# A seven-product tile's sixth token operand, high part too, moved 128 bytes; the mixer's order set anew

## The chip, the core and the metric

The kernel runs on one core of a Trainium2 chip. The metric is device time of one execution in microseconds; lower is better. Time is given as the median of three runs, and the profile is that of one further execution.

## What is computed

One decoder layer in float32 on 512 tokens of width 1024: a SwiGLU block, three parallel token mixers (sparse attention in three branches, a gated delta rule, cross-attention into a memory of 256 tokens) with sigmoid gates, and a second SwiGLU block. Cut to what matters here:

```python
def reference(x, mem, ...):
    h = swiglu(rms_norm(x, ffn1_pre_norm), ffn1_w_gate, ffn1_w_up, ffn1_w_down)
    x = x + 0.5 * rms_norm(h, ffn1_post_norm)
    u = rms_norm(x, mix_pre_norm)
    o_nsa, o_dn, o_mem = ...            # three mixers on u @ w_in
    gates = sigmoid(u @ w_branch_gate).reshape(b, s, 3, d)
    merged = (gates[:, :, 0] * (o_nsa @ w_branch_nsa)
              + gates[:, :, 1] * (o_dn @ w_branch_dn)
              + gates[:, :, 2] * (o_mem @ w_branch_mem))
    x = x + rms_norm(merged @ w_out, mix_post_norm)
    h = swiglu(rms_norm(x, ffn2_pre_norm), ffn2_w_gate, ffn2_w_up, ffn2_w_down)
    return x + 0.5 * rms_norm(h, ffn2_post_norm)
```

`swiglu` is `(silu(h @ w_gate) * (h @ w_up)) @ w_down` with a hidden width of 2816, that is 22 tiles of 128.

## The kernel before

Every float32 product is made of three products of rounded halves (`fp32r`): high by high, low by high, high by low (`mm3`, L117 to L119). ScalarE rounds a weight to its high part (L106), VectorE or GpSimd subtracts to get the low part (L109).

The gate and up products of a SwiGLU tile, and most of the branch gates, are done in another way: two blocks of weights against four blocks of tokens by seven products where eight would be plain (`fast_prods`, L424). Such a seven-product tile issues 7 x 12 matmuls of 128 x 128 weights with 256 token columns, all on L436. For each product and each of four slices `k`, three matmuls follow each other: `wh` by `th`, `wl` by `th`, `wh` by `tl`. The order of the products by token operand is 0, 5, 4, 1, 3, 6, 2; operand 6 (`T_T4`) goes with the weight block `S_A22` into the up half.

The weights of a tile (`fset`, `mset`, or the tiles `xth` and `xtl` used again as `fxth`, `fxtl`) begin 16 elements, 64 bytes, into their tile (`OFFW`, L317). The token operands are: the high parts in one tile `thi` of seven blocks of 4096 bytes (L376), the low parts in `txa`, `txb`, `tmth`, two blocks each, and the last one alone in `tmtl`, which begins 32 elements, 128 bytes, into its tile. So operand 6 has its high part at a multiple of 4096 bytes from the start of `thi`, and its low part 128 bytes off. The matmuls of the first SwiGLU block (`fast_phase`, L461, tiles 6 to 21) lie between 71 and 242 us, those of the second one between 1051 and 1210 us.

In the mixer, seven pairs of gate tiles (`pair`, L1421) use the same seven products: three token operands are cut from `uh`, `ul` (`xth`, `xtl`), four are sums made by `token_sums`, in `uhi` (which takes the place of the tile `KA`) with the low parts in `uxa`, `uxb` and `ulo`; `ulo` begins 128 bytes into its tile. In the middle of each pair two branch products of 512 columns are issued (`mid`). Those tiles lie between 792 and 923 us.

What runs between is a list of tasks, issued in the order of a list (`order`, `order2` and so on, read by `tasks`, L1163). `off` gives a task a head start in the scheduler's priorities; `pool` says how many of its loads leave the low part to GpSimd (2 is every second one, 0 none). The ones touched: `i` (projection `in_vs`), `C3` (`cmp_probs`), `M..` (`merge`, a gate, a branch product and their product added into `mg`), `G.` (`mem_q`), `W3`, `S...`, `P...` (pieces of the attention branches), `k0`, `p2` (memory keys, post-norm). Engines work their own queue in order; the scheduler lays the queues out beforehand.

Of the kernel before, what the change touches and what calls it, by code (L numbers as in the profile page):

```python
# [36 lines left out]
PRM = {'order': ['i', 'a', 'w', 'c01', 'h01', 'r0', 'c00', 'c10', 'c02', 'l0', 'h00', 'h02', 'c11', 'c12', 'k0', 'h10', 'c22', 'h12', 'h11', 'c21', 'r1', 'k1', 'l1', 'h21', 'h22', 'b0', 'e0', 'z', 'c20', 'r2', 'h20', 'c32', 'l2', 'c31', 'd00', 'k2', 'h31', 'r3', 'd01', 'l3', 'b1', 'd02', 'x0', 's00', 'e1', 'd10', 'c30', 'h32', 'x1', 'h30', 'd11', 's01', 's02', 's03', 'q3', 'p0', 'd12', 'o0', 'p1', 'k3', 'q0', 'p2', 'p3', 's10', 'p4', 'q1', 'p5', 's11', 'p6', 'p7', 's12', 's13', 'o1', 'q2', 'f'], 'dma': {'l': 'sync', 'b': 'sync', 'd': 'scalar', 'c': 'sync', 'r': 'sync'}, 'off': {'b0': 300, 'h31': 400, 'r1': 50, 'h32': 50, 'h11': 100, 'h12': 200, 'd10': 100, 'A01': 100, 'A10': 100, 'A11': 50, 'A20': 400, 'A31': 100, 'A21': 20, 'x0': 20, 'x1': 20, 'L': 200, 'S310': 400, 'S001': 400, 'S311': 400, 'A30': 100, 'r0': 400, 'd02': 20, 's11': 100, 'V20': 400, 'l3': 100, 'q1': 20, 'f': 100, 'l1': 50, 'h20': 100, 'h22': 100, 'r3': 50, 'P010': 50, 'y': 100, 'h02': 50, 'S101': 20, 'A00': 100, 'Q0': 50, 'Q1': 200, 'Q2': 50, 'Q3': 50, 'P110': 400, 'V31': 400, 'd01': 200, 'o0': 400, 'p0': 50, 'p2': 400, 'p4': 400, 'p5': 400, 'p6': 400, 'p7': 20, 'b1': 200, 'h01': 100, 'P201': 400, 'e0': 100, 'e1': 100, 'o1': 20, 'q0': 50, 'q2': 20, 'h21': 20, 'd11': 200, 'p3': 400, 'U0': 100, 'c11': 20, 's00': 200, 'P011': 400, 'M14': 200, 'c20': 50, 'k2': 20, 'M03': 20, 'V00': 400, 'V01': 400, 'V10': 400, 'V11': 400, 'V21': 400, 'V30': 400, 'l2': 200, 'h00': 400, 'G0': 20, 'S210': 20, 'P101': 200, 'i': 100, 'G2': 100, 'M11': 20, 'F2324': 200, 'S201': 100}, 'ph': 'e', 'po': 'ss', 'xpd': (0, 1, 2), 'order2': ['K1', 'K0', 'B', 'M10', 'Q0', 'C0', 'Q1', 'S000', 'S001', 'P000', 'C3', 'P001', 'C1', 'S010', 'P010', 'C2', 'S011', 'V00', 'Q2', 'S101', 'S100', 'P011', 'S110', 'V01', 'M12', 'P100', 'W0', 'P101', 'S111', 'Q3', 'P110', 'S200', 'V10', 'P111', 'S210', 'V11', 'P200', 'M14', 'M15', 'S201', 'P201', 'S211', 'W1', 'V20', 'P211', 'P210', 'V21', 'S301', 'W2', 'S300', 'S311', 'P301', 'M11', 'P300', 'L', 'M13', 'S310', 'V30', 'M16', 'G2', 'M17', 'G0', 'P311', 'P310', 'V31', 'W3'], 'order0': ['d0', 'p0', 'n0', 't0', 'd1', 'k2', 'p2', 'k0', 'p3', 'n1', 'v', 'k3', 'k1', 't1'], 'order3': ['s2', 's3', 's7', 's6', 's5', 's1', 's0', 's4', 'd00', 'd01', 'd11', 'g', 'p0', 'd10', 'n0', 'p1', 't0', 'n1'], 't3': (('mm', 'r'), ('e', 's')), 'pool': {'W2': 2, 's13': 3, 'k0': 0, 'k1': 0, 'k2': 0, 'k3': 2, 'p3': 1, 'C0': 1, 'C1': 0, 'C2': 0, 'C3': 2, 'S310': 0, 'L': 3, 'd11': 3, 'p0': 1, 'p1': 1, 'p2': 1, 'p4': 2, 'p5': 1, 'p6': 1, 'p7': 1, 'S311': 0, 'h01': 1, 'h00': 2, 'h02': 0, 'h10': 0, 'h11': 0, 'h12': 0, 'h22': 0, 'h21': 2, 'h20': 0, 'h31': 0, 'h30': 3, 'h32': 0, 'i': 2, 'P011': 2, 'c21': 0, 'd01': 2, 'S000': 0, 'S001': 0, 'S010': 0, 'S011': 0, 'S100': 0, 'S101': 0, 'S110': 0, 'S111': 0, 'S200': 0, 'S201': 0, 'S210': 0, 'S211': 0, 'S300': 0, 'S301': 0, 'M24': 2, 'G2': 2, 'A01': 0, 'M10': 0, 'M15': 2, 'M12': 2, 'M14': 2, 'M13': 2, 'M17': 2, 'M11': 2, 'M16': 2, 'M23': 0, 'M27': 3, 'M01': 2, 'M00': 2, 'M03': 0, 'M07': 2, 'M06': 1, 'M22': 2, 'M04': 2, 'M20': 2, 'M26': 2, 'M02': 0, 'M21': 2, 'M25': 2, 'M05': 2, 'c11': 1, 'o1': 3, 'P000': 2, 'P001': 1, 'P010': 2, 'P100': 2, 'P101': 2, 'P110': 2, 'P111': 2, 'P200': 2, 'P201': 2, 'P210': 2, 'P211': 2, 'P301': 0, 'P300': 3, 'P310': 1, 'P311': 2, 'c12': 0, 'b1': 1, 'x0': 0, 'x1': 0, 'V21': 0, 'c30': 0, 'c01': 0, 'c02': 0, 'c00': 0, 'c10': 0, 'c22': 0, 'c20': 0, 'c31': 3, 'c32': 0, 's01': 3, 'A31': 0, 'd12': 0, 'y': 2, 'G0': 2, 'G1': 2, 'G3': 0, 'U3': 0, 'W3': 2, 'r1': 2, 's12': 3, 'U2': 0, 'Q0': 2, 'Q1': 2, 'Q2': 2, 'Q3': 1, 's00': 3, 's02': 2, 's03': 3, 's10': 2, 's11': 3, 'e1': 2, 'd00': 1, 'U0': 0, 'U1': 0, 'l2': 0, 'd02': 2, 'K1': 3, 'V11': 0, 'V00': 2, 'r2': 0, 'l3': 3, 'T3': 0, 'F0001': 0, 'A21': 3}, 'pool3': {'d00': 3, 'd01': 3, 'd10': 0, 'd11': 0, 'p1': 2, 't1': 3, 't0': 3, 's5': 2, 's7': 2, 's1': 2, 's0': 2, 's3': 2, 's6': 2, 's2': 2, 's4': 2, 'q0': 1}, 'pool0': {'t0': 2}, 'off0': {'p3': 20, 'n1': 50, 'k2': 200, 'k1': 20, 'p2': 100, 'p0': 400}, 'off3': {'s1': 20, 's5': 200, 'g': 50, 't0': 200, 'd10': 200, 'p0': 200, 'n0': 200}, 'tt': ('e', 's'), 'order_s': ['w000', 't00', 'w010', 't01', 'P00', 'w110', 'y', 'w100', 't03', 't02', 'P10', 'w011', 'w001', 'P01', 'w111', 'R0', 'w101', 'F000', 'P11', 'x', 'n', 't10', 't12', 'F200', 't11', 'F101', 't13', 'F110', 'B', 'F211', 'F011', 'c'], 't0': ('e', 's'), 'rs': ((0, 0), (0, 0)), 'ra': (1, 1), 'warm': 8, 'pools': {'F000': 0, 'F101': 0, 'F200': 0, 'F011': 0, 'F110': 0, 'F211': 0, 'w10': 0, 'w11': 1, 't00': 0, 't01': 0, 't02': 0, 't03': 0, 't13': 0, 't10': 0, 't11': 0, 't12': 0, 'w00': 0, 'w01': 0, 'w000': 0, 'P01': 0}, 'ptc': 'vvs', 'cva': 'v', 'offs': {'t13': 100, 'R1': 400, 't03': 20, 't02': 20, 'w001': 100, 'w110': 20, 'R0': 200}, 'vnc': 's', 'sp3': 0, 'hsc': 'vv', 'sf2': 2, 'psc': 'vvvv', 'sp1': 0, 'vbs': 'v', 't1c': 'vs', 'sgv': 256, 'nset': 1, 'order4': ['T0', 'A00', 'A01', 'T1', 'G1', 'T2', 'T3', 'F0001', 'G3', 'M07', 'D0001', 'A10', 'A11', 'F0203', 'A30', 'A31', 'U1', 'D0203', 'U0', 'A20', 'U3', 'A21', 'F0405', 'U2', 'D0405', 'F0620', 'D0620', 'F2122', 'D2122', 'F2324', 'D2324', 'F2526', 'D2526', 'M27'], 'gon2': 0}  # L37


class Body:  # L40
# [1583 lines left out]
```

## Time and profile before

| | us |
|---|---|
| median of three runs | 1339.57 (1331.78, 1339.57, 1341.33) |
| the profiled execution | 1339.93 |
| its span, first to last instruction | 1338.1 |
| TensorE (PE) busy | 1304.5, 97% of the span |
| VectorE (DVE) busy | 960.9, 72% |
| ScalarE (ACT) busy | 739.6, 55% |

PE is TensorE's matmuls, PEld its weight loads. Busy time of PE counts the modelled length of each matmul; matmuls overlap, so the distance from one start to the next tells more than the length. PEclk is the clock that the chip granted, as a share of full speed.

### The profile page before, as it was taken

What the parts mean: (1) busy time and instruction counts of PE and PEld (TensorE: products, weight loads), DVE (VectorE), ACT (ScalarE), POOL (GpSimd) and SP (SyncE); (2) the same over time, 40 slices, a digit from 0 to 9 for tenths busy, and PEclk for the clock granted to TensorE, in tenths of its full rate; (3) what the DMA queues carried; (4) which work ended last, traced back from release to release, by engine and by line L of the source; (5) the groups of instructions that cost most, each with busy time, mean ns of one, the idle gap of its engine ahead of it and who ended that gap; (6) DMA issues with size and microseconds to landing.
All of it is one profiled execution on the core that took longest, in us unless ns stands there. A gap on an engine that the chain in (4) does not pass through costs nothing. (4 is left out here: it accounts for less than half of the span.)

```text
span 1338.1 us, 22370 instructions
## 1 busy us (share of the span) xinstructions
PE 1304.5 (97%) x8091; PEld 1133.7 (85%) x8091; DVE 960.9 (72%) x1857; ACT 739.6 (55%) x1591; POOL 132.0 (10%) x116
## 2 busy tenths in 40 slices
PE   8999999999999999999999999999999999999997
PEld 7889999887887778788777778888888999998886
DVE  6898876768567866846898466566687787766775
ACT  6566665767455644416555345444685556546652
POOL 0020000000012222003120211223100000000000
PEclk9999999999999999999999999999999999999999
DMA  7553331587654341334121331323745433317673
GB/s 239 190 162 117 105 118 42 177 261 240 193 178 131 102 119 45 84 109 130 45 63 40 94 118 57 95 95 114 271 151 161 139 95 112 110 32 268 195 224 108
DMA packets 106302, 178.35 MB, mean 133 GB/s; under 512 B 18780, under 2 KB 28368, under 8 KB 106192
## 3 DMA queue, kind: packets, MB, share of 16 engines
q1 hardware_dynamic: 105904, 176.67, 42.0%
q8 instruction: 63, 1.03, 0.3%
q14 instruction: 47, 0.39, 0.1%
q10 hardware_dynamic: 288, 0.26, 0.1%
HBM read 166.84 MB, written 10.01 MB: 132 GB/s over the span
## 5 line engine op out<-in xcount | busy, mean ns | idle before, releaser
L106 ACT CAST whi<-wraw 128x512 fp32r<-128x512 f32 (+1 forms) x286 | 173.4, 617 | 163.5 <-PE pfm L119 56.5
L109 DVE TENSOR_TENSOR wlo<-wraw,whi 128x512 fp32r<-128x512 f32 (+1 forms) x252 | 172.8, 693 | 77.1 <-ACT whi L106 71.9
L117 PE MATMUL pfm<-xth,whi 128*128 128x512 f32 x272 | 109.3, 404 | 2.5 <-ACT tg L1132 1.4
L118 PE MATMUL pfm<-xth,wlo 128*128 128x512 f32 x272 | 109.3, 404 | 0.5 <-DVE wlo L109 0.5
L119 PE MATMUL pfm<-xtl,whi 128*128 128x512 f32 x272 | 108.1, 400 | 0.0
L106 ACT CAST ringh<-ringr 128x512 fp32r<-128x512 f32 x82 | 49.9, 622 | 41.8 <-DMA ringr<-in_ffn_d_dram 8.9
L436 PE MATMUL smm<-thi,fset 128*128 128x256 f32 x384 | 69.1, 279 | 0.0
L109 DVE TENSOR_TENSOR wlo<-ringr,ringh 128x512 fp32r<-128x512 f32 x75 | 51.4, 690 | 20.8 <-PE acc_e L119 8.0
L109 POOL TENSOR_TENSOR wlo<-wraw,whi 128x512 fp32r<-128x512 f32 (+1 forms) x31 | 42.6, 1375 | 237.3 <-ACT whi L106 138.7
L117 PEld LDWEIGHTS pfm<-xth,whi 128*128 128x128 f32 x272 | 51.1, 188 | 13.7 <-ACT tg L1132 2.2
L456 DVE TENSOR_TENSOR up<-s,smm 128x256 f32<-128x256 f32 x32 | 13.5, 421 | 66.2 <-ACT se L451 66.2
L118 PEld LDWEIGHTS pfm<-xth,wlo 128*128 128x128 f32 x272 | 51.2, 189 | 10.2 <-issue 0.9
L119 PEld LDWEIGHTS pfm<-xtl,whi 128*128 128x128 f32 x272 | 51.1, 188 | 9.2 <-issue 0.4
L436 PEld LDWEIGHTS smm<-thi,fset 128*128 128x128 f32 x384 | 58.4, 188 | 0.2
L436 PE MATMUL smm<-thi,fxtl 128*128 128x256 f32 x192 | 53.7, 280 | 0.6 <-DVE fxtl L411 0.6
L436 PE MATMUL smm<-thi,fxth 128*128 128x256 f32 x192 | 53.5, 279 | 0.0
L436 PE MATMUL se<-thi,fset 128*128 128x256 f32 x256 | 46.0, 279 | 0.0
L1057 ACT ACTIVATE Pm<-Pm,nm 128x128 f32<-128x128 f32 (+1 forms) x64 | 35.7, 560 | 12.8 <-DVE nm L1056 12.5
L123 DVE TENSOR_TENSOR Hl<-H,Hh 128x256 fp32r<-128x256 f32 x88 | 35.0, 421 | 7.0 <-ACT Hh L122 5.4
L402 DVE TENSOR_TENSOR fs<-fq 128x1024 f32<-128x1024 f32 x32 | 39.0, 1220 | 0.1
L436 PEld LDWEIGHTS se<-thi,fset 128*128 128x128 f32 x256 | 38.9, 188 | 0.0
L436 PEld LDWEIGHTS smm<-thi,fxtl 128*128 128x128 f32 x192 | 36.0, 188 | 1.0 <-DVE fxtl L411 1.0
(611 smaller groups left out, 4255.8 us busy)
## 6 DMA issues: line engine op xcount, KB each, us to landing
wraw<-in_ffn_d_dram SPq DMA_DIRECT2D x94, 256.0 KB, 2.8
ringr<-in_ffn_d_dram SPq DMA_DIRECT2D x82, 256.0 KB, 3.0
fq<-in_ffn_g_dram SPq DMA_DIRECT2D x64, 256.0 KB, 2.8
fq<-in_ffn_u_dram SPq DMA_DIRECT2D x64, 256.0 KB, 3.1
wraw<-in_ffn_g_dram SPq DMA_DIRECT2D x34, 256.0 KB, 3.3
wraw<-in_ffn_u_dram SPq DMA_DIRECT2D x34, 256.0 KB, 3.4
woraw<-in_w_out_dram SPq DMA_DIRECT2D x32, 256.0 KB, 3.7
mfq<-in_w_gate_dram SPq DMA_DIRECT2D x28, 256.0 KB, 2.9
```

The source lines that it names most:

```text
L106: nc.scalar.copy(hi, raw)
L109: eng.tensor_tensor(lo, raw, hi.bitcast(F32), op=OP.subtract)
L117: t.matmul(out, lh, rh, start=first, stop=False)
L118: t.matmul(out, ll, rh, start=False, stop=False)
L119: t.matmul(out, lh, rl, start=False, stop=last)
L123: return self.nc.vector.tensor_tensor(lo, src, hi.bitcast(F32), op=OP.subtract)
L402: add = lambda *x: v.tensor_tensor(*x, op=OP.add)
L436: m = lambda x, y, **kw: te.matmul(out, x, y, skip_group_check=True, **kw)
L456: v.tensor_tensor(up[:, 256:], s7, a, op=OP.subtract)
L1057: nc.scalar.activation(pm, pm, AF.Exp, bias=nm[:, qb : qb + 1], scale=-1.0, accum_out=sm[:, qb : qb + 1])
```

## The change

The high part of operand 6 is shifted by 32 elements (128 bytes) as well. `thi` becomes one flat tile with 64 more elements, and its blocks a list. In the mixer the high part of the operand whose low part is `ulo` (number 1 of the four) goes to the end of `uhi`, also 128 bytes off a multiple of 1024; `KA`, whose place it takes, grows by 64 elements, 256 bytes. All that lies behind these tiles in their pools moves by 256 bytes.

```diff
-                nc.scalar.copy(self.thi[:, i], f[i])
-                q = v.tensor_tensor(self.tlo[i], f[i], self.thi[:, i].bitcast(F32), op=OP.subtract)
+                nc.scalar.copy(self.thi[i], f[i])
+                q = v.tensor_tensor(self.tlo[i], f[i], self.thi[i].bitcast(F32), op=OP.subtract)
...
-        self.thi = st.tile([P, 7, 4, 256], F32R, name="thi")
+        thi = st.tile([P, 7 * 1024 + 64], F32R, name="thi")
+
+        self.thi = [thi[:, 1024 * i + i // 6 * 32 :][:, :1024].rearrange("p (k t) -> p k t", k=4) for i in range(7)]
...
-                KA = ap_.tile([P, 8, SEQ], F32R, tag="KA", name="KA")
+                KA = ap_.tile([P, 8 * SEQ + 64], F32R, tag="KA", name="KA")[:, : 8 * SEQ].rearrange("p (k t) -> p k t", k=8)
...
-                        E["hi"] = ap_.tile([P, 4, 4, 256], F32R, tag="KA", name="uhi")
+                        hi = ap_.tile([P, 4 * 1024 + 64], F32R, tag="KA", name="uhi")
+                        E["hi"] = [hi[:, o : o + 1024].rearrange("p (k t) -> p k t", k=4) for o in (0, 3104, 1024, 2048)]
```

The other lines only change `thi[:, i]` to `thi[i]` and `E["hi"][:, k]` to `E["hi"][k]`. The lists of tasks change like this (one dictionary on one line, L37; old above, new below, cut to the neighbours):

```diff
 order2
-'S000', 'S001', 'P000', 'C3', 'P001'
+'S000', 'C3', 'S001', 'P000', 'P001'
-'P110', 'S200', 'V10', 'P111', 'S210', 'V11', 'P200', 'M14', 'M15'
+'P110', 'M14', 'S200', 'V10', 'P111', 'S210', 'V11', 'P200', 'M15'
-'S310', 'V30', 'M16', 'G2', 'M17', 'G0', 'P311', 'P310', 'V31', 'W3'
+'S310', 'G2', 'V30', 'M16', 'G0', 'P311', 'P310', 'V31', 'W3', 'M17'
 order4
-'F0001', 'G3', 'M07', 'D0001'
+'F0001', 'M07', 'G3', 'D0001'
 order0
-'k2', 'p2', 'k0', 'p3'
+'k2', 'k0', 'p2', 'p3'
 pool
-'i': 2
+'i': 0, 'q1': 3, 'o0': 0
 off
-'S310': 400
+'s12': 200, 'P301': 50, 'P311': 200, 'W3': 100
 offs
+'P11': 20
```

No task, matmul, copy or transfer is added or taken away.

## Rows read from the trace of the kernel before

**Rows 1.** The page: busy time, and the granted clock in forty slices.
```profile
PE 1304.5 (97%) x8091; PEld 1133.7 (85%) x8091; DVE 960.9 (72%) x1857; ACT 739.6 (55%) x1591; POOL 132.0 (10%) x116
...
PEclk9999999999999999999999999999999999999999
```

**Rows 2.** L436 by windows: us, PE busy (matmuls), PEld, PEclk, DMA share, GB/s.
```profile
110.00:160.00 50.00, 50.00 (x442) 50.00 (x441) 1.00 0.36 114
1100.00:1150.00 50.00, 50.00 (x427) 50.00 (x427) 1.00 0.33 106
```

**Rows 3.** Timeline, first block: start us, length us, engine, line, out<-in, tile, count.
```profile
151.43 0.39 PE L436 MATMUL smm<-thi,fset 128*128 128x256 f32 x2
151.66 0.28 PE L436 MATMUL smm<-txb,fset 128*128 128x256 f32 x1
151.77 0.39 PE L436 MATMUL smm<-thi,fset 128*128 128x256 f32 x2
...
152.79 0.39 PE L436 MATMUL ss<-thi,fset 128*128 128x256 f32 x2
...
154.19 0.40 PE L436 MATMUL se<-thi,fset 128*128 128x256 f32 x2
...
155.56 0.28 PE L436 MATMUL smm<-thi,fxth 128*128 128x256 f32 x1
...
171.94 0.39 PE L436 MATMUL ss<-thi,fset 128*128 128x256 f32 x2
```

**Rows 4.** Timeline, second block, the same products.
```profile
1136.67 0.40 PE L436 MATMUL smm<-thi,fset 128*128 128x256 f32 x2
...
1138.09 0.40 PE L436 MATMUL ss<-thi,fset 128*128 128x256 f32 x2
...
1139.50 0.40 PE L436 MATMUL se<-thi,fset 128*128 128x256 f32 x2
...
1157.88 0.40 PE L436 MATMUL ss<-thi,fset 128*128 128x256 f32 x2
```

**Rows 5.** Timeline, gate pairs of the mixer, around a break at 890.41.
```profile
890.05 0.40 PE L436 MATMUL dmm<-xth,mset 128*128 128x256 f32 x2
890.29 0.28 PE L436 MATMUL dmm<-xtl,mset 128*128 128x256 f32 x1
890.41 0.68 PE L436 MATMUL de<-xth,mset 128*128 128x256 f32 x2
...
891.73 0.39 PE L436 MATMUL de<-xth,mset 128*128 128x256 f32 x2
...
892.07 0.39 PE L436 MATMUL ds<-uhi,mset 128*128 128x256 f32 x2
...
906.27 0.40 PE L436 MATMUL dmm<-xth,mset 128*128 128x256 f32 x2
...
907.69 0.40 PE L436 MATMUL de<-xth,mset 128*128 128x256 f32 x2
```

**Rows 6.** Timeline, plain products with 256 columns ahead of the second block.
```profile
1002.05 0.28 PE L117 MATMUL pg<-xth,whi 128*128 128x256 f32 x1
1002.17 0.28 PE L118 MATMUL pg<-xth,wlo 128*128 128x256 f32 x1
1002.29 0.28 PE L119 MATMUL pg<-xtl,whi 128*128 128x256 f32 x1
```

**Rows 7.** Waits of PE between 700 and 812 us: us in total, times, longest.
```profile
PE de L436 <- DVE mset L416: 2.1, 1, 2.1
PE pfm L117 <- ACT mq L1294: 1.9, 1, 1.9
PE pfm L117 <- ACT tg L1132: 1.4, 1, 1.4
PE de L436 <- DVE mset L411: 1.2, 1, 1.2
```

**Rows 8.** Timeline around 805 us, ACT and DVE; idle before and its releaser in brackets.
```profile
804.51 1.22 DVE L402 TENSOR_TENSOR msum<-mfq 128x1024 f32<-128x1024 f32 x1 [1.93 <-DMA mfq<-in_w_gate_dram]
805.82 0.62 ACT L415 CAST mset<-msum 128x512 fp32r<-128x512 f32 x1 [2.30 <-DVE msum L402]
807.07 0.59 ACT L1294 ACTIVATE mq<-pfm 128x512 f32<-128x512 f32 x1
807.71 0.50 PE L117 MATMUL pfm<-onh,whi 128*128 128x512 f32 x1 [1.90 <-ACT mq L1294]
```

**Rows 9.** Windows, all engines: us, PE, PEld, DVE, ACT, POOL busy (count), PEclk, DMA.
```profile
385.00:410.00 25.00, 24.96 (x177) 23.29 (x176) 12.18 (x33) 13.86 (x37) 3.76 (x6) 1.00 0.49 145
600.00:700.00 100.00, 99.39 (x556) 77.72 (x555) 80.88 (x248) 62.02 (x170) 23.61 (x19) 1.00 0.28 80
```

**Rows 10.** All matmuls into `smm` and the pairs' `ds`, by tile: duration ns min/median/max, first and last start.
```profile
L436 PE MATMUL smm<-thi,fset x384: 276/281/281, 71.6 to 1197.2; 128*128 128x256 f32 x192
L436 PE MATMUL smm<-thi,fxth x192: 276/281/281, 90.6 to 1207.0; 128*128 128x256 f32 x192
L436 PE MATMUL ds<-uhi,mset x56: 276/281/682, 795.0 to 910.3; 128*128 128x256 f32 x56
```

More of the change, by code (lines that the diff above doesn't have):

```diff
@@ new lines @@
+PRM = {'order': ['i', 'a', 'w', 'c01', 'h01', 'r0', 'c00', 'c10', 'c02', 'l0', 'h00', 'h02', 'c11', 'c12', 'k0', 'h10', 'c22', 'h12', 'h11', 'c21', 'r1', 'k1', 'l1', 'h21', 'h22', 'b0', 'e0', 'z', 'c20', 'r2', 'h20', 'c32', 'l2', 'c31', 'd00', 'k2', 'h31', 'r3', 'd01', 'l3', 'b1', 'd02', 'x0', 's00', 'e1', 'd10', 'c30', 'h32', 'x1', 'h30', 'd11', 's01', 's02', 's03', 'q3', 'p0', 'd12', 'o0', 'p1', 'k3', 'q0', 'p2', 'p3', 's10', 'p4', 'q1', 'p5', 's11', 'p6', 'p7', 's12', 's13', 'o1', 'q2', 'f'], 'dma': {'l': 'sync', 'b': 'sync', 'd': 'scalar', 'c': 'sync', 'r': 'sync'}, 'off': {'b0': 300, 'h31': 400, 'r1': 50, 'h32': 50, 'h11': 100, 'h12': 200, 'd10': 100, 'A01': 100, 'A10': 100, 'A11': 50, 'A20': 400, 'A31': 100, 'A21': 20, 'x0': 20, 'x1': 20, 'L': 200, 'S001': 400, 'S311': 400, 'A30': 100, 'r0': 400, 'd02': 20, 's11': 100, 'V20': 400, 'l3': 100, 'q1': 20, 'f': 100, 'l1': 50, 'h20': 100, 'h22': 100, 'r3': 50, 'P010': 50, 'y': 100, 'h02': 50, 'S101': 20, 'A00': 100, 'Q0': 50, 'Q1': 200, 'Q2': 50, 'Q3': 50, 'P110': 400, 'V31': 400, 'd01': 200, 'o0': 400, 'p0': 50, 'p2': 400, 'p4': 400, 'p5': 400, 'p6': 400, 'p7': 20, 'b1': 200, 'h01': 100, 'P201': 400, 'e0': 100, 'e1': 100, 'o1': 20, 'q0': 50, 'q2': 20, 'h21': 20, 'd11': 200, 'p3': 400, 'U0': 100, 'c11': 20, 's00': 200, 'P011': 400, 'M14': 200, 'c20': 50, 'k2': 20, 'M03': 20, 'V00': 400, 'V01': 400, 'V10': 400, 'V11': 400, 'V21': 400, 'V30': 400, 'l2': 200, 'h00': 400, 'G0': 20, 'S210': 20, 'P101': 200, 'i': 100, 'G2': 100, 'M11': 20, 'F2324': 200, 'S201': 100, 's12': 200, 'P301': 50, 'P311': 200, 'W3': 100}, 'ph': 'e', 'po': 'ss', 'xpd': (0, 1, 2), 'order2': ['K1', 'K0', 'B', 'M10', 'Q0', 'C0', 'Q1', 'S000', 'C3', 'S001', 'P000', 'P001', 'C1', 'S010', 'P010', 'C2', 'S011', 'V00', 'Q2', 'S101', 'S100', 'P011', 'S110', 'V01', 'M12', 'P100', 'W0', 'P101', 'S111', 'Q3', 'P110', 'M14', 'S200', 'V10', 'P111', 'S210', 'V11', 'P200', 'M15', 'S201', 'P201', 'S211', 'W1', 'V20', 'P211', 'P210', 'V21', 'S301', 'W2', 'S300', 'S311', 'P301', 'M11', 'P300', 'L', 'M13', 'S310', 'G2', 'V30', 'M16', 'G0', 'P311', 'P310', 'V31', 'W3', 'M17'], 'order0': ['d0', 'p0', 'n0', 't0', 'd1', 'k2', 'k0', 'p2', 'p3', 'n1', 'v', 'k3', 'k1', 't1'], 'order3': ['s2', 's3', 's7', 's6', 's5', 's1', 's0', 's4', 'd00', 'd01', 'd11', 'g', 'p0', 'd10', 'n0', 'p1', 't0', 'n1'], 't3': (('mm', 'r'), ('e', 's')), 'pool': {'W2': 2, 's13': 3, 'k0': 0, 'k1': 0, 'k2': 0, 'k3': 2, 'p3': 1, 'C0': 1, 'C1': 0, 'C2': 0, 'C3': 2, 'S310': 0, 'L': 3, 'd11': 3, 'p0': 1, 'p1': 1, 'p2': 1, 'p4': 2, 'p5': 1, 'p6': 1, 'p7': 1, 'S311': 0, 'h01': 1, 'h00': 2, 'h02': 0, 'h10': 0, 'h11': 0, 'h12': 0, 'h22': 0, 'h21': 2, 'h20': 0, 'h31': 0, 'h30': 3, 'h32': 0, 'i': 0, 'P011': 2, 'c21': 0, 'd01': 2, 'S000': 0, 'S001': 0, 'S010': 0, 'S011': 0, 'S100': 0, 'S101': 0, 'S110': 0, 'S111': 0, 'S200': 0, 'S201': 0, 'S210': 0, 'S211': 0, 'S300': 0, 'S301': 0, 'M24': 2, 'G2': 2, 'A01': 0, 'M10': 0, 'M15': 2, 'M12': 2, 'M14': 2, 'M13': 2, 'M17': 2, 'M11': 2, 'M16': 2, 'M23': 0, 'M27': 3, 'M01': 2, 'M00': 2, 'M03': 0, 'M07': 2, 'M06': 1, 'M22': 2, 'M04': 2, 'M20': 2, 'M26': 2, 'M02': 0, 'M21': 2, 'M25': 2, 'M05': 2, 'c11': 1, 'o1': 3, 'P000': 2, 'P001': 1, 'P010': 2, 'P100': 2, 'P101': 2, 'P110': 2, 'P111': 2, 'P200': 2, 'P201': 2, 'P210': 2, 'P211': 2, 'P301': 0, 'P300': 3, 'P310': 1, 'P311': 2, 'c12': 0, 'b1': 1, 'x0': 0, 'x1': 0, 'V21': 0, 'c30': 0, 'c01': 0, 'c02': 0, 'c00': 0, 'c10': 0, 'c22': 0, 'c20': 0, 'c31': 3, 'c32': 0, 's01': 3, 'A31': 0, 'd12': 0, 'y': 2, 'G0': 2, 'G1': 2, 'G3': 0, 'U3': 0, 'W3': 2, 'r1': 2, 's12': 3, 'U2': 0, 'Q0': 2, 'Q1': 2, 'Q2': 2, 'Q3': 1, 's00': 3, 's02': 2, 's03': 3, 's10': 2, 's11': 3, 'e1': 2, 'd00': 1, 'U0': 0, 'U1': 0, 'l2': 0, 'd02': 2, 'K1': 3, 'V11': 0, 'V00': 2, 'r2': 0, 'l3': 3, 'T3': 0, 'F0001': 0, 'A21': 3, 'q1': 3, 'o0': 0}, 'pool3': {'d00': 3, 'd01': 3, 'd10': 0, 'd11': 0, 'p1': 2, 't1': 3, 't0': 3, 's5': 2, 's7': 2, 's1': 2, 's0': 2, 's3': 2, 's6': 2, 's2': 2, 's4': 2, 'q0': 1}, 'pool0': {'t0': 2}, 'off0': {'p3': 20, 'n1': 50, 'k2': 200, 'k1': 20, 'p2': 100, 'p0': 400}, 'off3': {'s1': 20, 's5': 200, 'g': 50, 't0': 200, 'd10': 200, 'p0': 200, 'n0': 200}, 'tt': ('e', 's'), 'order_s': ['w000', 't00', 'w010', 't01', 'P00', 'w110', 'y', 'w100', 't03', 't02', 'P10', 'w011', 'w001', 'P01', 'w111', 'R0', 'w101', 'F000', 'P11', 'x', 'n', 't10', 't12', 'F200', 't11', 'F101', 't13', 'F110', 'B', 'F211', 'F011', 'c'], 't0': ('e', 's'), 'rs': ((0, 0), (0, 0)), 'ra': (1, 1), 'warm': 8, 'pools': {'F000': 0, 'F101': 0, 'F200': 0, 'F011': 0, 'F110': 0, 'F211': 0, 'w10': 0, 'w11': 1, 't00': 0, 't01': 0, 't02': 0, 't03': 0, 't13': 0, 't10': 0, 't11': 0, 't12': 0, 'w00': 0, 'w01': 0, 'w000': 0, 'P01': 0}, 'ptc': 'vvs', 'cva': 'v', 'offs': {'t13': 100, 'R1': 400, 't03': 20, 't02': 20, 'w001': 100, 'w110': 20, 'R0': 200, 'P11': 20}, 'vnc': 's', 'sp3': 0, 'hsc': 'vv', 'sf2': 2, 'psc': 'vvvv', 'sp1': 0, 'vbs': 'v', 't1c': 'vs', 'sgv': 256, 'nset': 1, 'order4': ['T0', 'A00', 'A01', 'T1', 'G1', 'T2', 'T3', 'F0001', 'M07', 'G3', 'D0001', 'A10', 'A11', 'F0203', 'A30', 'A31', 'U1', 'D0203', 'U0', 'A20', 'U3', 'A21', 'F0405', 'U2', 'D0405', 'F0620', 'D0620', 'F2122', 'D2122', 'F2324', 'D2324', 'F2526', 'D2526', 'M27'], 'gon2': 0}
@@ L472, in fast_phase @@
         self.fast_load(*gu(f0 + 3), self.sets[1], (quads[1], sums))
-        T = [(self.thi[:, i], self.tlo[i]) for i in range(7)]
+        T = [(self.thi[i], self.tlo[i]) for i in range(7)]
         for f in range(f0 + 2, FT):
@@ L1412, in sum4 @@
                             homes()
-                        self.token_sums(k, uh, ul, E["tt"], E["hi"][:, k], E["lo"][k])
+                        self.token_sums(k, uh, ul, E["tt"], E["hi"][k], E["lo"][k])
                     def gates(br, j, br2, j2):
@@ L1423, in pair @@
                         T = [(q(uh, i, k), q(ul, i, k)) for i, k in ((0, 0), (1, 0), (1, 1))]
-                        T += [(E["hi"][:, k], E["lo"][k]) for k in (0, 1, 3, 2)]
+                        T += [(E["hi"][k], E["lo"][k]) for k in (0, 1, 3, 2)]
                         b = [self.bank(t, "d" + t) for t in ("e", "s", "mm", "o")]
```

1 line of the change is left out of this document (removed).

## The prediction

> **What bounds the kernel now.** I read the page first. PE is busy 97% of the span, and the clock row shows nines in all forty slices [rows 1]; so the kernel ends when TensorE has worked off its list, and a gain must come from faster matmuls or from fewer holes between them. Busy time can't tell the first: I next took the matmuls of L436 by windows. The windows of both SwiGLU blocks are busy for 50.00 of 50.00 us at a granted clock of 1.00 (2.4 GHz), yet the first block gets 442 matmuls into its window and the second one 427 [rows 2]. The same program, the same shapes, 3.5% more time in the second.
>
> The timeline shows where. In the first block three matmuls take 151.77 - 151.43 = 0.34 us, twelve (one product) 152.79 - 151.43 = 1.36 us, that is 113 ns from start to start [rows 3]. In the second block the same product takes 1138.09 - 1136.67 = 1.42 us, 118 ns a matmul [rows 4]. Two speeds, and in neither block is the engine waiting for anything that the profile shows. Nor is it the place of one operand alone: in the gate pairs, the three matmuls up to 890.41 take 0.36 us, then something disturbs the stream (0.68), and from 891.73 to 892.07 three take 0.34; at 906.27 the same product takes 907.69 - 906.27 = 1.42 us again [rows 5]. The stream keeps the step it has fallen into until something jolts it. There is a third step: the plain products of 256 columns, whose weights have no 64-byte offset, go at 1002.17 - 1002.05 = 0.12 us [rows 6]. So where operands lie in bytes seems to matter, and the stream also remembers.
>
> Operand 6, whose low part lies 128 bytes off, is where the two blocks differ least. In the first block its product takes 154.19 - 152.79 = 1.40 us and the next one 155.56 - 154.19 = 1.37, and then the stream is back at 1.36 [rows 3]: some 0.05 us lost per tile. In the second block it takes 1139.50 - 1138.09 = 1.41 us [rows 4], and nothing changes after it. So the half-shifted operand disturbs a quick stream a little, and doesn't free a slow one.
>
> **The change, part by part.** *The shift of operand 6 in the second block.* No instruction is added. With both parts off, all twelve matmuls of that product meet their weights at one new distance in bytes, where before eight did so at the old and four at the new one. Either this knocks the stream out of the 118 ns step at every tile, or not. If it does, a tile costs what it costs in the first block. Two tiles there take 171.94 - 152.79 = 19.15 us, 9.575 each [rows 3]; in the second block 1157.88 - 1138.09 = 19.79, 9.895 each [rows 4]. The difference is 0.32 us. The high weights of `fset` meet `smm` in 384 matmuls, of `fxth` in 192 with one of the two weight parts [rows 10]; with three products of eight such matmuls per tile that is 384 / 24 = 16 tiles of `fset` in both blocks, and as many of the other weight set (whose two parts are counted apart): 16 tiles per block. Gain: 16 x 0.32 = 5.1 us. Bounds: 0 if the stream stays slow.
>
> *The same in the gate pairs.* `ds` takes eight high-part matmuls per pair, 56 in all [rows 10], so seven pairs; a slow one loses the same 0.32. About one of seven goes quick by itself, as after 890.41 [rows 5]. Gain 6 x 0.32 = 1.9 us, bounds 0 and 2.2.
>
> *The shift in the first block.* The stream is quick there already. Operand 6's own product may go to 1.36 (gain 16 x 0.05 = 0.8) or to twelve matmuls at 0.12, 1.44 us (loss 16 x 0.04 = 0.6, by [rows 6]). I take 0, since two thirds of it already run mixed, near the middle. The rival below is that it drops the stream into the slow step.
>
> *The 256 bytes that other tiles move by* (the pairs' weights, the loads ahead of the second block): 64 and 256 bytes are the steps in which the code lays things out, and no row shows what 256 does. If it mattered, every third load ahead of the second block would be the most: of the two tiles in two halves, 2 x 2 x 2 x 24 = 192 matmuls at 0.120 [rows 6], a third gain 0.007, 0.4 us. I take 0 and keep 0.4 both ways.
>
> *The order of the mixer.* PE's work stays; only holes can close or open. Those next to the moved tasks are the four waits between 700 and 812 us, 2.1 + 1.9 + 1.4 + 1.2 = 6.6 us [rows 7]. M17 goes behind W3 and M07 ahead of G3: both put ready matmuls close to the first pair, whose weights come late from VectorE (the waits on `mset`, 3.3 us). But the work they bring there is taken from somewhere else, and their own evictions queue on ScalarE and VectorE ahead of the pair's. The 1.9 us wait shows what can go wrong: the copy of `mq` (G3, 0.59 us) stood on ScalarE behind a cast that waited 2.30 us for `msum`, which had waited 1.93 us for its DMA, and the branch product behind it needed the bank that the copy frees [rows 8]. With G3 later, that copy is no earlier. Bounds: a gain of 6.6 if all four close, a loss of two more waits of the largest size, 4.2. I take a gain of 0.5, near nothing, since most of each wait is one engine's queue that is as long as before.
>
> *The rest.* `i` gives its four GpSimd subtractions to VectorE: in its stretch PE is busy 24.96 of 25 us and VectorE only 12.18 [rows 9], so PE's matmuls hide it; uncovered it would be four of GpSimd's instructions there at 3.76 / 6 = 0.63 us, 2.5 us. C3, M14 and the new head starts lie where PE is 99.39 of 100 us busy [rows 9]: nothing to close, and up to 0.6 to lose or gain. k0 ahead of p2 and P11's head start the same way. Together 0.
>
> **The sum.** 1339.9 (the profiled execution, 1338.1 of it span, 0.4 above the median) - 5.1 - 1.9 - 0.5 = 1332.4 us.
>
> The three runs before lie at 1331.78, 1339.57 and 1341.33. A kernel that can run at two speeds would show such a spread: the lowest is 8.1 us below the mean of the others (1340.45), and 5.1 + 1.9 is 7.0. That is a hint that whole executions go either way already, no proof.
>
> **The rivals.**
>
> *B. The place in bytes decides nothing; the slow step stays.* For it: the half shift leaves the second block slow for all sixteen tiles [rows 4], and a stall, not an operand, freed the pair at 890.41 [rows 5]. Against it: 0.120 against 0.113 between weights at two offsets [rows 3, 6]. Time: 1339.9 - 0.5 = 1339.4. The Trainium skill, "SBUF — State Buffer", section "Who interferes with whom", speaks for this rival: it gives TensorE two independent read ports, one for the moving operand and one for weight loads, and says it waits on no one; by that an address couldn't change the step. The trace agrees only in part, as two steps at one granted clock [rows 2] are more than that page has.
>
> *C. The jolt works in one of the two places.* In the second block only: 1339.9 - 5.1 - 0.5 = 1334.3; in the pairs only, 1337.5. For it: pairs and blocks have their weights at other places, and branch products break the pairs up.
>
> *D. Slower: the first block falls into the slow step.* Its place is operand 6 there. Today the stream leaves that product and is back at 1.36 after one product [rows 3]; if the wholly shifted product hands it on at 118 ns, and nothing frees it, as in the second block [rows 4], sixteen tiles lose 0.32. It decides if the product that follows operand 6 takes 1.41 and not 1.37. With the second block still slow: 1339.9 + 5.1 = 1345.0. For it: both steps sustain themselves. Against it: an operand that lies elsewhere has so far been left behind within one product.
>
> *E. The mixer's order opens waits.* G3's late copy twice holds up a branch product: two more waits of 2.1 us [rows 7], 1339.9 + 4.2 = 1344.1.
>
> **How the numbers follow.** The forecast (both streams freed) 0.45; B 0.29; C 0.12; D 0.08; E 0.06. The forecast's own range is 1326 (all four waits closed) to 1336 (operand 6 at 0.12 in all tiles, some loss in the mixer). The range for 8 in 10 reaches from 1327.5 to 1341.5: it takes in most of the forecast, B and C, and leaves out D, E and the lowest end. About 1% is what a measurement of this kernel can tell from no change: 1326.2 and 1353.0. Below the first lies only the forecast with nearly all of the mixer's 6.6 us: 0.06. Above the second only D and E together with more: 0.02. Within: 0.92.
>
> **What would show it.** Right: 442 matmuls in a 50 us window of the second block as in the first, and a tile of 9.6 us; pairs with three matmuls in 0.34; the first block unchanged. The order's part is seen in the waits of PE around 800 us, in sum between 0 and 11 us against 6.6. Wrong: 427 in the second block (B), 427 in the first (D), or the span moving by more than 3 us between 340 and 790 us, where I count nothing.

## Result, and the profile after

The changed kernel takes 1329.76 us (median of 18 runs, 1324.47 to 1337.19) against 1337.91 us before (18 runs, 1331.78 to 1345.76): a ratio of 0.994, 95% interval 0.9923 to 0.9958, so 8 us less. The forecast was 1332.4 us, 7.5 us below the profiled execution, in a range of 1327.5 to 1341.5. The sum came out close, but not its terms, and the experiments below are about which of them did it. The profiled execution of after took 1327.85 us; its page:

```profile
PE 1299.2 (98%) x8091; PEld 1129.2 (85%) x8091; DVE 959.7 (72%) x1860; ACT 738.6 (56%) x1591; POOL 126.6 (10%) x113
...
PEclk8999999999999999999999999999999999999999
```

The same 8091 matmuls [rows 1]; TensorE is busy 5.3 us less. The lines of `fast_prods` and all below it have moved down by one, so L436 is L437 here. Its matmuls by windows (us, PE busy, PEld, PEclk, DMA share, GB/s):

```profile
110.00:160.00 50.00, 50.00 (x441) 50.00 (x440) 1.00 0.37 116
1100.00:1150.00 50.00, 50.00 (x441) 50.00 (x440) 1.00 0.34 107
```

Against 442 and 427 [rows 2], both blocks now go at the quick step. In the timeline of the second block, one product start each (start us, length us, engine, line, out<-in, tile, count):

```profile
1145.38 0.39 PE L437 MATMUL smm<-thi,fset 128*128 128x256 f32 x2
...
1146.74 0.40 PE L437 MATMUL ss<-thi,fset 128*128 128x256 f32 x2
...
1148.15 0.40 PE L437 MATMUL se<-thi,fset 128*128 128x256 f32 x2
...
1149.52 0.28 PE L437 MATMUL smm<-thi,fxth 128*128 128x256 f32 x1
...
1150.88 0.28 PE L437 MATMUL sr<-thi,fxth 128*128 128x256 f32 x1
```

A product takes 1146.74 - 1145.38 = 1.36 us where it took 1.42 [rows 4]; the shifted one takes 1.41, the next 1.37, and then 1.36 again. That is the picture of the quick stream in the first block before [rows 3], so the whole shift disturbs a quick stream about as the half one did.

The pairs, in the timeline of one of them:

```profile
867.16 0.40 PE L437 MATMUL de<-xth,mset 128*128 128x256 f32 x2
...
868.58 0.40 PE L437 MATMUL ds<-uhi,mset 128*128 128x256 f32 x2
...
872.74 0.40 PE L437 MATMUL de<-uhi,mset 128*128 128x256 f32 x2
872.97 0.28 PE L437 MATMUL de<-ulo,mset 128*128 128x256 f32 x1
...
874.15 0.40 PE L437 MATMUL dmm<-xth,mset 128*128 128x256 f32 x2
...
875.52 0.39 PE L437 MATMUL de<-uhi,mset 128*128 128x256 f32 x2
...
876.88 0.39 PE L437 MATMUL do<-uhi,mset 128*128 128x256 f32 x2
...
878.24 0.40 PE L117 MATMUL pfm<-omth,whi 128*128 128x512 f32 x1
```

In a pair the shifted operand is not number 6 but number 4, the third product, straight behind the first branch product. Ahead of it a product takes 1.42 us, the shifted one (`ulo`) 1.41, and the three behind it 1.37, 1.36, 1.36. Then the second branch product follows, of 512 columns, and behind it the stream is slow again. So three of seven products are quick in each of the six later pairs; in the first one other matmuls stand between the products, and one is quick.

Of the waits of PE between 700 and 812 us [rows 7] none is left. In the stretch of the pairs, 785 to 925 us, one is (us in total, times, longest); it stood there before too, as L1137:

```profile
PE pfm L117 <- DVE tg L1138: 1.4, 1, 1.4
```

Where the time went between the two profiled executions, by the starts of the same matmuls: at the last matmul of the first block after is 0.3 us ahead, at the first matmul of the pairs 1.3, at the last one 8.3, at the first seven-product matmul of the second block 7.9, at its last one 12.7, at the end 12.0. So the pairs gave 7.0 us, 5.2 of it the three waits of [rows 7] that lay in them, and the second block 4.9. The first block gave nothing. The wait for `tg` of 1.4 us, which lay at 744, is gone too, but the stretch from the first block to the pairs got only 1.1 us shorter (550.6 to 549.5).

### The profile page after: what moved, and what is told of

Read it like the earlier page. It is cut to its first block, busy times and chain, and to the rows that moved or that the text cites. A ratio compares the mean times of both kernels' runs of the same rounds, so it can differ in the third digit from the quotient of the medians.

```text
span 1326.1 us, 22368 instructions
## 1 busy us (share of the span) xinstructions
PE 1299.2 (98%) x8091; PEld 1129.2 (85%) x8091; DVE 959.7 (72%) x1860; ACT 738.6 (56%) x1591; POOL 126.6 (10%) x113
## 5 line engine op out<-in xcount | busy, mean ns | idle before, releaser
L437 PE MATMUL smm<-thi,fset 128*128 128x256 f32 x384 | 67.9, 276 | 0.0
L109 POOL TENSOR_TENSOR wlo<-wraw,whi 128x512 fp32r<-128x512 f32 x28 | 38.1, 1360 | 229.2 <-ACT whi L106 165.1
L437 PEld LDWEIGHTS smm<-thi,fset 128*128 128x128 f32 x384 | 57.9, 188 | 0.2
L437 PE MATMUL smm<-thi,fxtl 128*128 128x256 f32 x192 | 53.2, 277 | 0.6 <-DVE fxtl L412 0.6
L437 PE MATMUL smm<-thi,fxth 128*128 128x256 f32 x192 | 53.0, 276 | 0.0
L437 PE MATMUL se<-thi,fset 128*128 128x256 f32 x256 | 45.2, 276 | 0.0
L1058 ACT ACTIVATE Pm<-Pm,nm 128x384 f32<-128x384 f32 (+2 forms) x64 | 35.6, 558 | 14.5 <-DVE nm L1057 14.0
L437 PEld LDWEIGHTS se<-thi,fset 128*128 128x128 f32 x256 | 38.6, 188 | 0.0
L437 PEld LDWEIGHTS smm<-thi,fxtl 128*128 128x128 f32 x192 | 36.0, 188 | 1.0 <-DVE fxtl L412 1.0
```

What stands on the lines that cost most here:

```text
L109: eng.tensor_tensor(lo, raw, hi.bitcast(F32), op=OP.subtract)
L437: m = lambda x, y, **kw: te.matmul(out, x, y, skip_group_check=True, **kw)
L1058: nc.scalar.activation(pm, pm, AF.Exp, bias=nm[:, qb : qb + 1], scale=-1.0, accum_out=sm[:, qb : qb + 1])
```

## Experiments

The theory after the result: the order of the mixer closed the waits; the whole shift frees the slow stream in the second block and in part of the pairs. The rival: the step of a block is set by something else, and the shift has no part in it.

**The shift alone, and the order alone.** The code of after with the lists of before:

```diff
-PRM = {... the lists of after ...}
+PRM = {... the lists of before ...}
```

> The shift of operand 6 with the old order of tasks. If the shift frees the stream (the forecast): the second block's tile takes 9.58 us as in the changed kernel, not 9.90, its 16 tiles give 4.8 to 5.1 us; in the gate pairs the four products that follow the shifted operand take 1.36, some 1.3 us; the four waits of TensorE between 700 and 812 us stay at 6.6 us; in sum about 6 us faster than before. If the order of the mixer set the stream's step (a stall at another moment): tile 9.90, time as before.

Measured: 1340.01 us (12 runs, 1330.04 to 1343.87) against 1339.1 before; ratio 0.9993, interval 0.9968 to 1.0019. Its windows and its waits between 700 and 960 us:

```profile
110.00:160.00 50.00, 50.00 (x426) 50.00 (x426) 1.00 0.31 107
1100.00:1150.00 50.00, 50.00 (x441) 50.00 (x440) 1.00 0.33 112
```

```profile
PE pfm L117 <- ACT mq L1295: 3.1, 1, 3.1
PE de L437 <- DVE mset L417: 2.1, 1, 2.1
PE de L437 <- DVE mset L412: 2.0, 2, 1.3
PE pfm L117 <- ACT tg L1133: 1.4, 1, 1.4
```

The shift alone brings nothing that can be measured. The second block is quick here, but the first one, quick before, is slow through all its tiles, with the shifted operand in each of them. The shifted product passes a slow stream on as slow. The waits of the order of before are all there, that for `mq` 1.2 us longer than in [rows 7], and the pairs take 133.3 us, although three products in each of the later six are quick.

The other half is before's code with the lists of after:

```diff
-PRM = {... the lists of before ...}
+PRM = {... the lists of after ...}
```

> The new order of tasks with operand 6 only half shifted. If the two parts of the change are independent: the second block's tile takes 9.90 us, the pairs' products 1.41, the four waits of 6.6 us between 700 and 812 us are gone, the stretch of the pairs is some 5 us shorter, and the time is 4 to 6 us below before. If the order only fits the shifted layout: less than 2 us. If the order frees the stream: tile 9.58 and the whole gain.

Measured: 1332.35 us (12 runs, 1324.48 to 1335.77), ratio 0.9947, interval 0.9926 to 0.9969. The first block is quick, the second slow (427 matmuls in the window from 1100), the pairs are slow behind `ulo` too, and the four waits are gone. The first and the last matmul of its pairs:

```profile
790.32 0.40 PE L436 MATMUL de<-xth,mset 128*128 128x256 f32 x2
...
915.15 0.28 PE L436 MATMUL dmm<-xtl,mset 128*128 128x256 f32 x1
```

That is 124.8 us from start to start, against 130.8 before and 123.8 after. So the order does 6.0 us in the pairs, the shift 1.0 more there (one profile against one; after once more, below, takes 124.0), and the order alone, at 0.9947, gives nearly all of the whole change's 0.994. The stretch from the first block to the pairs takes 550.5 us here, as before, so the 1.1 us that after saves there isn't shown to come from the order.

**Which move of the order.** Before, with one task moved each (M17 from ahead of `G0` to behind W3; M07 from behind G3 to ahead of it):

```diff
-'M16', 'G2', 'M17', 'G0', 'P311', 'P310', 'V31', 'W3'
+'M16', 'G2', 'G0', 'P311', 'P310', 'V31', 'W3', 'M17'
```

> The kernel before with M17 moved to the end of its list and nothing else. If M17's ready matmuls fill the stretch ahead of the first pair: the waits of TensorE on mset (2.1 and 1.2 us) go, and the one of 1.4 us behind L1132 with them. If the swap of M07 and G3 does it: all four waits stay.

Measured: 1328.89 us (one run), with both blocks quick in its profile where before has one; the pairs take 126.2 us. Its waits from 700 to 812 us, and the issues of loads on SP's queue:

```profile
PE pfm L117 <- ACT tg L1132: 1.4, 1, 1.4
PE de L436 <- ACT do L447: 1.2, 1, 1.2
```

```profile
768.10 3.88 SPq L105 DMA_DIRECT2D wraw<-in_w_gate_dram  x2
773.67 0.33 SPq L403 DMA_DIRECT2D mfq<-in_w_gate_dram  x1
...
775.52 5.83 SPq L105 DMA_DIRECT2D wraw<-in_w_br_dram  x3
```

Before, the same queue and VectorE's wait for what it brings:

```profile
763.13 1.48 SPq L105 DMA_DIRECT2D wraw<-in_w_gate_dram  x2
767.44 16.53 SPq L105 DMA_DIRECT2D wraw<-in_w_br_dram  x4
784.06 0.38 SPq L403 DMA_DIRECT2D mfq<-in_w_gate_dram  x1
```

```profile
789.23 1.94 DVE L402 TENSOR_TENSOR msum<-mfq 128x1024 f32<-128x1024 f32 x1 [3.64 <-DMA mfq<-in_w_gate_dram]
```

This is the cause of the waits for `mset`. The raw weights of the first pair (`mfq`) stood on SP's queue behind four loads of branch weights, whose issue stretched over 16.53 us, and VectorE, which makes `mset` of them, itself waited 3.64 us for the transfer. With M17 behind W3 the loads of the pair are issued ahead of these, at 773.67 and not at 784.06, 10.4 us earlier, and the waits for `mset` and `mq` are gone (5.2 us); a new one of 1.2 takes some of it back, and the wait for `tg` stays. In after the first of those loads starts at 770.0.

```diff
-'F0001', 'G3', 'M07', 'D0001'
+'F0001', 'M07', 'G3', 'D0001'
```

> The kernel before with M07 ahead of G3 and nothing else. If G3's late copy on ScalarE is what the swap mends: the wait of 1.9 us on mq goes and the others stay. If, as the prediction had it, the copy comes no earlier: 1.9 us stay or grow.

Measured: 1335.82 us (one run), the pairs 131.6 us, 0.8 more than before. Its longest waits from 700 to 812 us:

```profile
PE pfm L117 <- ACT mq L1294: 3.9, 1, 3.9
PE de L436 <- DVE mset L411: 1.5, 1, 1.5
```

Alone this move makes the wait for `mq` 2.0 us longer: with G3 later, its copy still stands behind the casts of the next pair's weights [rows 8]. In after that costs nothing, since there those weights come early. In both of these kernels the operand is shifted in its low part alone, as before, and in both the second block is quick (441 in the window from 1100). That counts against the shift as the cause.

**The same program once more.** The changed kernel unaltered, in another session:

> The changed kernel once more, for its profile alone. If the stall in each block's first tile leaves the step to chance, execution by execution: any of the four combinations of quick and slow blocks, with a time that fits: 1326 for two quick blocks, some 1331 for one, 1336 for none. If the changed layout fixes the step: both blocks quick, as in its first profile.

Measured: 1333.17 us (one run). Its windows, and the start of its second block:

```profile
110.00:160.00 50.00, 50.00 (x441) 50.00 (x441) 1.00 0.32 111
1100.00:1150.00 50.00, 50.00 (x427) 50.00 (x427) 1.00 0.32 111
```

```profile
1046.95 0.38 PE L437 MATMUL smm<-thi,fxtl 128*128 128x256 f32 x1 [0.26 <-DVE fxtl L412]
1047.17 0.40 PE L437 MATMUL smm<-thi,fset 128*128 128x256 f32 x2
...
1048.59 0.40 PE L437 MATMUL se<-thi,fset 128*128 128x256 f32 x2
```

The same place in the profile of after:

```profile
1046.96 0.39 PE L437 MATMUL smm<-thi,fxtl 128*128 128x256 f32 x1 [0.26 <-DVE fxtl L412]
1047.18 0.40 PE L437 MATMUL smm<-thi,fset 128*128 128x256 f32 x2
...
1048.56 0.39 PE L437 MATMUL se<-thi,fset 128*128 128x256 f32 x2
```

One program, the same matmuls at the same times within 0.01 us, the same stall of 0.26 us on `fxtl`, and behind it the first product takes 1.42 us in one execution and 1.38 in the other. The stream keeps that step to the end of the block: 158.7 us from first to last matmul here, 153.8 in after, 158.7 before. The second block's 4.9 us are thus not a gain that the change secures; it fell out that way in one execution. Each block has one stall of this kind, in its first tile, where TensorE waits for the low weights of the second (0.38 us in the first block). Ahead of it the products take 1.41 in every profile, and behind it the step stands. By profile (first block, second block): before quick, slow; after quick, quick; the shift alone slow, quick; the order alone quick, slow; M17 and M07 alone quick, quick; after again quick, slow. Counting the kernels below as well, where their weights begin 64 bytes in and the product behind the stall is unshifted, 10 of 12 blocks are quick with the whole shift, 6 of 8 with the half one, 2 of 2 with none. So few can't exclude that the shift changes the odds; the shift alone at 0.9993 says what it was worth in all.

**No shift at all, and the weights elsewhere.** After, with neither part of the operand shifted, in blocks and pairs:

```diff
-    self.thi = [thi[:, 1024 * i + i // 6 * 32 :][:, :1024]... for i in range(7)]
+    self.thi = [thi[:, 1024 * i :][:, :1024]... for i in range(7)]
-    last = self.cp.tile([P, 1056], F32R, tag="mtl", ...)[:, 32:]...
+    last = self.cp.tile([P, 1056], F32R, tag="mtl", ...)[:, :1024]...
-    E["hi"] = [... for o in (0, 3104, 1024, 2048)]
+    E["hi"] = [... for o in (0, 3072, 1024, 2048)]
-    E["lo"][1] = ms.tile([P, 1056], F32R, name="ulo")[:, 32:]...
+    E["lo"][1] = ms.tile([P, 1056], F32R, name="ulo")[:, :1024]...
```

> The changed kernel with operand 6 not shifted at all, neither part. If the stream keeps whatever step it fell into until something jolts it: each block runs wholly at 1.36 a product or wholly at 1.41 from its first stall on, with no tile between; at 1.36 throughout a tile takes 9.52 us, 0.05 less than with the shift, at 1.41 it takes 9.90. If the shift is what makes the quick step possible at all: both blocks at 1.41, some 10 us slower than the changed kernel.

Measured: 1334.96 us (10 runs, 1324.61 to 1337.85), ratio 0.9961, interval 0.9935 to 0.9987. Its profile is that of its fastest run: both blocks quick (443 and 444 in the windows), the product of operand 6 too; all pairs but the first slow.

```profile
1143.19 0.39 PE L437 MATMUL ss<-thi,fset 128*128 128x256 f32 x2
...
1144.55 0.39 PE L437 MATMUL se<-thi,fset 128*128 128x256 f32 x2
```

With no shift the product of operand 6 takes 1144.55 - 1143.19 = 1.36 us in a quick stream, with the shift 1.41 (after, from 1146.74). So a block can go quick with no shift whatever, and the place in bytes does decide how long a product takes. Its other nine runs lie 5 to 13 us higher.

The same with the weights 192 bytes into their tile and not 64:

```diff
-    OFFW = 16
+    OFFW = 48
```

> No operand shifted; instead all weights of seven-product tiles begin 192 bytes into their tile, not 64. So every product meets its weights at the distance that only operand 6 has in the changed kernel (there its product takes 1.41 us). If the distance in bytes sets the step: all products 1.41, tile 9.90 in both blocks, with no way out. If only the change from one distance to another matters: both steps occur, 9.52 or 9.90 per tile.

Measured: 1336.14 us (one run), with 427 and 426 in the windows and 1.41 us for every product, in blocks and pairs, behind stalls too. At this distance between weights and tokens no quick product was seen; but this is one profile, with two stalls, and at 64 bytes 4 of the 22 blocks counted above were slow as well, so that it gives only the slow step isn't shown. The Trainium skill, "SBUF — State Buffer", section "Who interferes with whom", gives TensorE two read ports that are independent of each other. That alone doesn't account for the step: at one granted clock of 1.00 the same product took 1.36 us unshifted and 1.41 shifted. Whether the ports have to do with it no run here shows.

**The shift on the product right behind the stall.** After, with operand 4 shifted in the SwiGLU blocks in place of operand 6:

```diff
-    self.thi = [thi[:, 1024 * i + i // 6 * 32 :][:, :1024]... for i in range(7)]
+    self.thi = [thi[:, o : o + 1024]... for o in (0, 1024, 2048, 3072, 6176, 5120, 4096)]
-    self.tlo = [lo[i // 2][:, i % 2] for i in range(6)] + [last]
+    self.tlo = [lo[i // 2][:, i % 2] for i in range(4)] + [last, lo[2][:, 0], lo[2][:, 1]]
```

> The changed kernel with operand 4 shifted in both SwiGLU blocks, not operand 6 (the pairs as changed). Operand 4 is the first product after the stall on L412 in each block's first tile. If the stall leaves the step to chance and the shift only passes the step on that it finds, but a stream that enters the shifted product afresh, from a stall or from 512-column matmuls, leaves it quick: both blocks run at 1.36 in every execution, the median lies at the low end of the changed kernel's runs, 1324 to 1327 us, and the runs spread less. If the shift frees a slow stream wherever it stands: the same median as the changed kernel, 1330 us. If it matters that operand 6 is the one: slower, 1335 us.

Measured: 1334.8 us (12 runs, 1331.31 to 1336.38), ratio 0.9985 to a before of 1335.66 in that session, interval 0.9968 to 1.0002. Both blocks are slow from the stall on (426 and 427), and no shifted product on the way frees them. Neither the 1324 to 1327 nor the 1330 us came; 1335 did, but no run shows that operand 6 is what matters. The runs lie within 5.1 us, where before and after have 14 and 13. This fits a layout that has lost the chance of a quick block; that it is slow in every run was not seen, as one was profiled.

**Jolting the stream in a block.** After, with matmuls of 512 columns whose result nobody reads, ahead of operand 6 in the second seven-product tile of each block; six of them, and two:

```diff
+        for i in range(6 if first else 0):
+            te.matmul(wide, hi[:, self.S_A22, :P], T[0][0][:, 0:2]..., start=True, stop=True, ...)
```

> The changed kernel with six more matmuls of 512 columns, whose result nobody reads, in the second seven-product tile of each SwiGLU block, straight ahead of the shifted operand 6 and behind the stall (12 x 0.227 = 2.7 us more work). It copies what frees the stream in every gate pair: 512 columns, then the shifted product. If that is the mechanism: both blocks run at 1.36 from their second tile on in every execution; the runs crowd within 5 us, around 1326 + 2.7 = 1329 us, with none above 1334. If the step stays what the stall made it: the runs spread over 12 us as those of the changed kernel, and lie 2.7 us higher, median 1332 to 1333.

> The same with two such matmuls per block (0.9 us in all). If two wide matmuls are enough to enter the shifted product afresh: runs crowded around 1327 us, better than the changed kernel's median of 1330. If not: spread as the changed kernel, 0.9 us higher.

Measured, six: 1329.59 us (10 runs, 1326.48 to 1334.31), ratio 0.9954 (0.9935 to 0.9974); two: 1327.58 us (8 runs, 1325.11 to 1331.74), ratio 0.9939 (0.9918 to 0.996), against 1334.92 before. The timeline of the second block with two (`fast_prods` has its matmuls on L438 there):

```profile
1061.44 0.28 PE L438 MATMUL smm<-thi,fxth 128*128 128x256 f32 x1
...
1061.78 0.28 PE L438 MATMUL smm<-thi,fxth 128*128 128x256 f32 x1
...
1062.12 0.62 PE L455 MATMUL sr<-thi,fxth 128*128 128x512 f32 x2
1062.58 0.28 PE L438 MATMUL ss<-thi,fxth 128*128 128x256 f32 x1
...
1063.95 0.28 PE L438 MATMUL se<-thi,fxth 128*128 128x256 f32 x1
...
1065.36 0.40 PE L438 MATMUL smm<-thi,fset 128*128 128x256 f32 x2
...
1072.43 0.40 PE L438 MATMUL ss<-thi,fset 128*128 128x256 f32 x2
...
1073.84 0.40 PE L438 MATMUL se<-thi,fset 128*128 128x256 f32 x2
...
1080.65 0.28 PE L438 MATMUL smm<-thi,fxth 128*128 128x256 f32 x1
...
1082.01 0.28 PE L438 MATMUL ss<-thi,fxth 128*128 128x256 f32 x1
```

Ahead of the wide matmuls the stream is quick here (1061.78 - 1061.44 = 0.34 for three); the shifted product straight behind them is quick too (1063.95 - 1062.58 = 1.37), which no shifted product is elsewhere. Then the stream is slow (1065.36 - 1063.95 = 1.41), stays so for a tile, and behind the next shifted product, which begins at 1072.43, it is quick and stays quick: 1082.01 - 1080.65 = 1.36. The first block shows the same, and so does the profile with six. So here the wide matmuls made a quick stream slow for a tile, and a shifted operand freed it, as one does in the pairs, and as it does not behind the stall on `fxtl`. It seems that there are two kinds of slow stream. What was to be tested, a block that its stall left slow, is in neither profile, as all four blocks came out of the stall quick. The runs lie within 7.8 us (six) and 6.6 us (two), closer than the 12.7 of after but not within 5, and one with six is above 1334; so that the wide matmuls free a block in every execution isn't shown. The kernel with two matmuls has the lowest median of all, but its ratio is that of the change itself, and it has not been timed beside it.

**Both branch products early in a pair.** After, with the second one ahead of the shifted operand too, so that it isn't followed by slow products:

```diff
-        for f in mid[:1]:
+        for f in mid:
...
-        for f in mid[1:]:
-            f()
```

> The changed kernel with both branch products of a gate pair issued ahead of the shifted operand, so that a pair has one break and not two. If 512-column matmuls followed by an unshifted product make the step slow, and followed by the shifted one quick: six of a pair's seven products take 1.36, not four, and 7 x 2 to 3 x 0.053 = 0.7 to 1.1 us are saved, unless the earlier second branch waits for its bank. If each product has its own step: no change in the products' times.

Measured: 1331.99 us (12 runs, 1329.45 to 1335.88), ratio 0.9962, interval 0.9942 to 0.9982. Three pairs have six quick products of seven and two have five, where after has three; and yet the pairs take 129.3 us, 5.5 more than in after. The longest waits from 785 to 925 us:

```profile
PE de L437 <- ACT do L448: 2.7, 2, 1.4
PE pmt L1115 <- DVE Pm L1111: 1.5, 2, 0.8
```

More products are quick, and new waits cost more than that: ScalarE's `do` and the attention weights `Pm` are now needed earlier than they are ready. TensorE is idle 5.3 us in the pairs, 1.5 in after; where the rest of the 5.5 us goes isn't shown.

## Why the prediction was right, and where it was not

*The total.* 7.5 us were forecast and 8.1 came between the medians. The terms as the profiles bear them out are -6.0 for the order in the pairs, -1.0 for the shift there, about 0 for the second block, and -1.1 between the first block and the pairs, whose cause isn't shown: 8.1 in all. So two terms were off by at least 5.5 and by 5.1 us in opposite directions, and the sum was close by luck.

*The order of the mixer* (-0.5, bounds -6.6 and +4.2). This step failed. It measured -6.0 us in the pairs, near the bound of -6.6: all four waits closed [rows 7]. The failing sentence is that most of each wait "is one engine's queue that is as long as before". It took VectorE for what was late. VectorE waited itself, for a transfer, and the transfer was late because its issue stood on SP's queue behind loads of the tasks ahead. [rows 8] showed this for the second pair (`msum` behind its DMA for 1.93 us); I read it as a reason for the `mq` copy's wait and didn't follow it back to the queue of loads. Moving M17 moves its loads too, and M17 alone closed the three waits in the pairs. What I said on G3 held where it was tested alone (3.9 us in place of 1.9), and was undone by the early weights in the whole change. So rival E lost by a cause that the prediction didn't see.

*The second block* (-5.1). The size of a step was right: 158.7 against 153.8 us in two executions of one program, 4.9 us. Its cause was wrong. "Either this knocks the stream out of the 118 ns step at every tile, or not" left out a third case, which the sentence on a stream that keeps its step "until something jolts it" allowed: that each block comes out of one stall and keeps the step that it has then. After has a quick block and a slow block in two executions with one and the same layout, and blocks with half a shift or none were quick as well. The sentence on the runs of before, that whole executions go either way, held (its 8.1 us is 1340.45 - 1331.78 = 8.7, further from the 7.0 it is set beside), and should have been given more weight than a hint: with it a profile of one execution can't price this term.

*The pairs* (-1.9). Mechanism right, size off: -1.0 us. The shifted product frees the three products behind it in a pair, not all seven, as the second branch product makes the stream slow again. The pair after 890.41 [rows 5], counted as quick by itself, was so only up to its first branch product: the product that begins at 897.87 takes 1.42 there.

*The first block* (0) held in after. Rival D, that the block falls into the slow step, came about in the profile of the shift alone, with 426 in its window; but this too is the draw at the stall, not what the shift does to a quick stream, which it leaves quick.

*Rival B* (the bytes decide nothing) is refuted by one product in a quick stream, 1.36 us without the shift and 1.41 with it, though for this change it came nearest: the shift alone measured 0.9993. *The 256 bytes and the rest* (0): from 340 to 790 us the two profiles part by 0.8 us, within the 3 us that were allowed.

**What stays open.** What decides at the stall whether the stream is quick or slow isn't shown; within 0.01 us the timelines are the same ahead of it. Nor is it shown why a shifted product frees the stream behind wide matmuls and not behind that stall. The traces in whole nanoseconds hold a hint on the first: with weights at 64 bytes and an unshifted product behind the stall, the start of the stalled matmul lies 536, 536 and 537 ns behind the one before it in the three slow second blocks and 537 to 539 in the eight quick ones; 654 in the one slow first block and 655 to 659 in the ten quick ones. So no slow block's stall is longer than a quick one's, and they differ by a few nanoseconds at most. That this decides isn't shown. Nor is it shown that the chance per block alone makes the spread of the runs. The shift alone has four runs at 1330.04 to 1335.18 and eight at 1339.58 to 1343.87; their medians lie 8.2 us apart, more than one block's step of 4.9, and the profiled run, among the eight, has one block quick already. The runs were not profiled one by one.

## To carry to other kernels

When a wait names an engine, follow the instruction that it waits for one step further back: if that one waited for a transfer, the place of its issue on the queue of loads is what a moved task changes. Where the same matmuls run at two speeds within one profile, profile the same program twice before an edit is given credit for either speed. Undo each part of a mixed change by itself: here the part that looked like the change brought some 1 us, and the reordered list 6 to 7.
